# The first norm's root moved behind the first products, with the first two projections walked half by half and the gates' chain turned onto 128 partitions

## The chip, the cores and the metric

The kernel runs on one core of one Trainium2 chip. The core has a matrix engine (PE, with PEld for its weight loads), a vector engine (DVE), a scalar engine (ACT), a general engine (POOL) and a sync engine (SP), which here only issues DMAs. Each engine takes its instructions in the order in which they stand in the program and waits, one instruction at a time, for what they need. The metric is the device time of one execution in microseconds (us), as a median of several runs.

## The reference

A token block of 256 tokens of width 1024 passes one hybrid layer and two further layers. The change touches the beginning of the first:

```python
hdn = rms_norm(x, g_mix_pre)          # x * rsqrt(mean(x^2) + eps) * g
proj = hdn @ w_in                     # 1024 x 3080
aq, ak, av, mq, mk, mv, mo, mi, mf = split(proj)   # 512,512,512,256,256,512,512,4,4
att = causal_attention(rope(aq), rope(ak), av)     # 8 heads of 64
ig, lf = mi + b_igate, log_sigmoid(mf + b_fgate)   # per token and head
hm = mlstm(mq, mk / 8, mv, ig, lf)                 # 4 heads; uses cumsum(lf), running maximum
hm = rms_norm(hm) * g_mlstm_out * sigmoid(mo)
x = x + rms_norm(concat(att, hm) @ w_out, g_mix_post)
x = x + rms_norm(square(relu(rms_norm(x) @ w_up)) @ w_down)
```

After it come two layers with modulation by `ada_w`, differential attention, a convolution branch and a gated MLP of width 2816. All of it is float32.

## The kernel before, in words

**Products.** Every float32 product is made of three fp32r matmuls: high part of the activation by high part of the weight, high by low, low by high (`mm3`, L282 to L284). Where tokens are the stationary side, one matmul is 128 x 512 wide (`mm_tok`); where weights are, 128 x 256 (`mm_col`). The activations stand transposed in a tile `T` (name `hT`), 8 pieces `k` of 128 rows, high and low part.

**The stream of weights.** All large weights come as a list of units of 1 MB (`plan`), in halves of 512 KB. `issue_dma` (L189, on SP) loads a half into one of 8 buffers `raw`. `split` makes of it `whi` on ACT (L199) and `wlo` on POOL (L203) or on DVE (L205); a counter (`rot`) gives three of four to POOL. `pump` steps through the plan as far as the 9 buffers for `whi` and `wlo` let it; each step issues one later DMA. Units of `ada_w` in the plan are no weights for PE: DVE works them off itself (L713).

**Order.** The order on every engine is that of the program's text. Side work is written as generators: queues `fills`, `fills2` and others, of which `tick` takes one step after each used half. So what the text emits beside which half of the weights is set by counts such as `GATES` (steps put before the gates' chain starts).

**The first stage.** SP issues x's first block, the gains' row, 4 halves of `w_in`, x's second block, then more halves; behind 16 halves stand the small loads (positions, norm rows, `dw_conv_w`, the gates' columns `wif`, their biases `bif`, the lambdas), then the stream goes on. Per token block, the norm takes squares and the root (L469, `pre_scale`), multiplies x by it (L474, L475), transposes (L494), multiplies by the gain (L500, L502) and splits into high and low (L552, L553): `pre_trans`. `a2_block` then runs `aq` and `ak`: token block 0 over all 8 halves, then block 1 over the 8 halves that are still held. After it come the blocks `av`, `mq`, `mk`, `mv`, `mo` in the order `ORDER1`.

**Side work of that stage.** `rotary` (L601 on) makes sines and cosines. `setup` (L650 on) transposes the small rows. `mlstm_gates` (L852 on) makes the gates' 36 x 256 product (24 matmuls against `wif`), then the log-sigmoid and its cumulative sum on 4 partitions x 256 tokens on DVE (L867 to L885), two steps of it between other things per used half. `attention1` (L919) makes the scores (L791, L792), the softmax (its last step on DVE is `P`, L945), the transposes of the probabilities (L808) and the products; it starts once `aq` and `ak` are turned by `rope` and transposed (L783). `mlstm` (L954) begins by transposing the gates' two rows.

Of the kernel before, what the change touches and what calls it, by code (L numbers as in the profile page):

```python
# [11 lines left out]
FT = mybir.dt.float32  # L12
# [15 lines left out]
HB, RB, XB = 9, 8, 4  # L28
SLACK = 2
HOLD0, HOLDZ, HOLDF = 8, 8, 7  # L30
# [10 lines left out]
ST = (1, 1, 4, 1)  # L41
EARLY, CHAIN, TWO = 1, 3, 0
GATES = 3
# [12 lines left out]
def tile_hybrid_then_diff(ctx: ExitStack, tc: tile.TileContext, I, out: bass.AP):  # L56
# [232 lines left out]

    def mm_col(o, xT, k, w, kk, cs, start, stop):  # L290
        h, lo = (xT[0], xT[1]) if isinstance(xT, list) else (xT[:, 0], xT[:, 1])
        mm3(o, w[0][:, kk, cs], w[1][:, kk, cs], h[:, k, :], lo[:, k, :], start, stop)

    def a_block(tag, xT):
        acc = [acc_tile(), acc_tile()]
        for i in range(4):
            w = take(tag)
            for kk in range(2):
                k = 2 * i + kk
                for t in range(2):  # L300
                    mm_tok(acc[t], xT, k, t, w, kk, slice(0, 512), k == 0, k == 7)
# [7 lines left out]
    def a2_block(seq, xT, before, evac, hold):  # L309
# [7 lines left out]
        def half(out, t, b, k0, kn, w):  # L317
            for kk in range(kn):
                k = k0 + kk
                mm_tok(out[b][:, 0:1024 // kn], xT, k, t, w, kk, slice(0, 1024 // kn), k == 0, k == 7)  # L320
# [122 lines left out]

    ident = cst.tile([128, 128], FT, name="ident")
# [7 lines left out]
    ones = cst.tile([128, 128], FT, name="ones")  # L452
    V.memset(ones, 1.0)
# [105 lines left out]

    p = ps_tile()  # L560
    T.transpose(p[:, 0:8], row0, ident[0:8, 0:8])
    col0 = cst.tile([128, 8], FT, name="col0")
    V.tensor_copy(col0, p[:, 0:8])
    hT = new_T()
    xn = {0: pre_scale(0, ST[0])}
    pump(ST[1])
    run(pre_trans(0, xn[0], hT, lambda j: col0[:, j:j + 1], None))
    pump(ST[2])
    xn[1] = pre_scale(1, ST[3])

    posi = cst.tile([128, 2, 2], I32, name="posi")
    small(posi[:, 0, :], I["positions"].rearrange("o (t p) -> p (o t)", p=128))
    small(posi[:, 1, :], I["positions_2"].rearrange("o (t p) -> p (o t)", p=128))
    ROW = {}
    n0 = 0
    for nm, src in (("g_mlp_pre", I["g_mlp_pre"]), ("c", I["c_2"]), ("n1", I["norm1_g_2"]),
                    ("n2", I["norm2_g_2"]), ("lg", I["conv_ln_g_2"]), ("lb", I["conv_ln_b_2"]),
                    ("cb", I["dw_conv_b_2"]), ("sg", I["subln_g_2"]), ("go", I["g_mlstm_out"])):
        v = src.rearrange("l (j p) -> (l j) p", p=128)
        small(rows[n0:n0 + v.shape[0], :], v)  # L580
        ROW[nm] = n0
        n0 += v.shape[0]
    small(rowa[0:96, :], I["ada_b_2"].rearrange("l (j p) -> (l j) p", p=128))
    small(crow[0:31], I["dw_conv_w_2"].rearrange("l k o c -> k l (o c)"))
    wv = w1.rearrange("(k p) n -> p k n", p=128)
    small(wif[:, :, 0:4], wv[:, :, 3072:3076])
    small(wif[:, :, 32:36], wv[:, :, 3076:3080])
    bif = cst.tile([4, 2], FT, name="bif")
    small(bif[:, 0:1], I["b_igate"].rearrange("l h -> h l"))
    small(bif[:, 1:2], I["b_fgate"].rearrange("l h -> h l"))  # L590
    for i, nm in enumerate(("lambda_q1_2", "lambda_k1_2", "lambda_q2_2", "lambda_k2_2")):
        src = I[nm]
        small(lamr[:, :, i, :], bass.AP(tensor=src.tensor, offset=src.offset, ap=[[0, 128], [64, 2], [1, 64]]))

    pump(2)
# [5 lines left out]
    def rotary():  # L601
# [25 lines left out]
        for s in range(2):  # L627
# [11 lines left out]
                  for _ in range(2))  # L639
    nlam = cst.tile([128, 2], FT, name="nlam")  # L640
# [9 lines left out]
    def setup():  # L650
        G.memset(mask, 0.0)
# [26 lines left out]
        set_up.append(1)  # L678
        yield
        lst = st_tile()  # L680
# [171 lines left out]
    def mlstm_gates():  # L852
# [7 lines left out]
        gw = xn_tile((4, 4, 256))  # L860
        ig, zf, e, s = (gw[:, i, :] for i in range(4))
        s2 = b = e
# [33 lines left out]
    def evac(t, acc):  # L896
# [8 lines left out]
        if t == 0:  # L905
            fills.append(setup())
# [496 lines left out]
```

## Time and profile before

| | |
|---|---|
| median of 3 runs | 1123.03 us (1116.99, 1123.03, 1123.46) |
| the profiled execution's own time | 1118.56 us |
| its span, first to last instruction | 1116.8 us |
| busy: PE, DVE, ACT, POOL | 94%, 61%, 50%, 63% of the span |
| granted TensorE clock, mean | 0.979 of full speed |

The span is one execution; the 1.8 us beside it are the start and the end around it. An engine's share of the span is a mean over many stages. The stage that the change touches is the first 90 us, and there the idle stretches of PE, and what ended them, say more than the shares.

### The profile page before, as it was taken

What the parts mean: (1) busy time and instruction counts of PE and PEld (TensorE: products, weight loads), DVE (VectorE), ACT (ScalarE), POOL (GpSimd) and SP (SyncE); (2) the same over time, 40 slices, a digit from 0 to 9 for tenths busy, and PEclk for the clock granted to TensorE, in tenths of its full rate; (3) what the DMA queues carried; (4) which work ended last, traced back from release to release, by engine and by line L of the source; (5) the groups of instructions that cost most, each with busy time, mean ns of one, the idle gap of its engine ahead of it and who ended that gap; (6) DMA issues with size and microseconds to landing.
All of it is one profiled execution on the core that took longest, in us unless ns stands there. A gap on an engine that the chain in (4) does not pass through costs nothing.

```text
span 1116.8 us, 17204 instructions
## 1 busy us (share of the span) xinstructions
PE 1052.6 (94%) x6435; PEld 927.4 (83%) x6435; DVE 683.3 (61%) x1161; ACT 559.8 (50%) x931; POOL 709.0 (63%) x419
## 2 busy tenths in 40 slices
PE   5969989999999899989999998989999899999997
PEld 4756778998897778988798998878889888999995
DVE  2694535999964387835569688645875455642323
ACT  5535556434455546674633333446466555443441
POOL 5753455665686597665566655757958467567671
PEclk9988999999999999999999999999999899999998
DMA  9562244999996375454599989836535366775631
GB/s 317 138 205 94 76 156 146 320 337 311 343 314 202 95 207 171 151 170 152 150 310 314 333 317 340 310 131 191 176 125 165 121 197 203 239 246 188 197 108 38
DMA packets 170191, 231.82 MB, mean 208 GB/s; under 512 B 10983, under 2 KB 110525, under 8 KB 170107
## 3 DMA queue, kind: packets, MB, share of 16 engines
q1 hardware_dynamic: 169979, 230.71, 63.1%
q8 instruction: 50, 0.82, 0.3%
q14 instruction: 34, 0.28, 0.1%
q0 software_dynamic: 128, 0.02, 0.0%
HBM read 229.63 MB, written 1.06 MB: 207 GB/s over the span
## 4 chain that ended last, share of the span: by engine, by line
PE 53%; DVE 15%; POOL 9%; issue 8%; ACT 7%; DMA 6%; SPq 1%; POOLq 0%; DVEq 0%; ACTq 0%
PE bank L282 16%; PE bank L283 16%; PE bank L284 16%; POOL wlo L203 8%; DVE bank L713 3%; ACT whi L199 3%; DMA raw<-in_w_ffn_in_dram 3%; DVE wlo L205 2%; DMA raw<-in_w_down_dram 2%; SPq L426 1%; DVE modc L738 1%; ACT xn L469 1%; PE bank L792 1%; PE bank L791 1%; DMA raw<-in_w_ffn_out_dram 1%
## 5 line engine op out<-in xcount | busy, mean ns | idle before, releaser
L203 POOL TENSOR_TENSOR wlo<-raw,whi 128x1024 fp32r<-128x1024 f32 x262 | 653.6, 2518 | 308.2 <-ACT whi L199 271.5
L199 ACT ACTIVATE whi<-raw 128x1024 fp32r<-128x1024 f32 x332 | 337.2, 1053 | 78.6 <-DMA raw<-in_w_ffn_in_dram 28.4
L282 PE MATMUL bank<-T,whi 128*128 128x256 f32 x1072 | 309.4, 289 | 6.0 <-ACT sc L1347 2.8
L284 PE MATMUL bank<-T,wlo 128*128 128x256 f32 x1072 | 304.6, 284 | 0.0
L283 PE MATMUL bank<-T,whi 128*128 128x256 f32 x1072 | 304.5, 284 | 0.0
L282 PEld LDWEIGHTS bank<-T,whi 128*128 128x128 f32 x1072 | 206.4, 193 | 13.8 <-issue 5.9
L283 PEld LDWEIGHTS bank<-T,whi 128*128 128x128 f32 x1072 | 206.5, 193 | 1.1
L284 PEld LDWEIGHTS bank<-T,wlo 128*128 128x128 f32 x1072 | 206.5, 193 | 0.0
L205 DVE TENSOR_TENSOR wlo<-raw,whi 128x1024 fp32r<-128x1024 f32 x70 | 126.3, 1805 | 91.3 <-ACT whi L199 91.0
L283 PE MATMUL bank<-wlo,T 128*128 128x512 f32 (+1 forms) x432 | 170.3, 394 | 11.4 <-POOL wlo L203 11.4
L282 PE MATMUL bank<-whi,T 128*128 128x512 f32 (+1 forms) x432 | 173.6, 402 | 3.0 <-ACT T L552 1.5
L284 PE MATMUL bank<-whi,T 128*128 128x512 f32 (+1 forms) x432 | 169.4, 392 | 0.0
L713 DVE SCALAR_TENSOR_TENSOR bank<-raw,cact,bank 128x512 f32<-128x512 f32 x168 | 126.8, 755 | 7.1 <-DMA raw<-in_ada_w_dram 1.8
L282 PE MATMUL bank<-whi,AB 128*128 128x512 f32 x304 | 120.7, 397 | 0.0
L284 PE MATMUL bank<-whi,AB 128*128 128x512 f32 x304 | 120.0, 395 | 0.0
L283 PE MATMUL bank<-wlo,AB 128*128 128x512 f32 x304 | 119.9, 394 | 0.0
L283 PEld LDWEIGHTS bank<-wlo,T 128*128 128x128 f32 x432 | 82.9, 192 | 29.7 <-POOL wlo L203 14.2
L1155 DVE SCALAR_TENSOR_TENSOR bank<-cu,cw,bank 128x256 f32<-128x256 f32 x232 | 104.4, 486 | 4.1
L282 PEld LDWEIGHTS bank<-whi,T 128*128 128x128 f32 x432 | 82.8, 192 | 23.2 <-ACT T L552 2.9
L284 PEld LDWEIGHTS bank<-whi,T 128*128 128x128 f32 x432 | 82.7, 191 | 17.5 <-DVE T L553 0.5
L552 ACT ACTIVATE AB<-bank 128x512 fp32r<-128x512 f32 (+1 forms) x49 | 26.0, 538 | 108.3 <-DVE bank L1351 63.7
L284 PEld LDWEIGHTS bank<-whi,AB 128*128 128x128 f32 x304 | 57.2, 188 | 13.4
(264 smaller groups left out, 1164.1 us busy)
## 6 DMA issues: line engine op xcount, KB each, us to landing
raw<-in_w_in_dram SPq DMA_DIRECT2D x96, 512.0 KB, 5.1
raw<-in_ada_w_dram SPq DMA_DIRECT2D x96, 512.0 KB, 7.4
raw<-in_w_ffn_in_dram SPq DMA_DIRECT2D x88, 512.0 KB, 4.7
raw<-in_w_ffn_out_dram SPq DMA_DIRECT2D x44, 512.0 KB, 5.2
raw<-in_w_up_dram SPq DMA_DIRECT2D x32, 512.0 KB, 5.5
raw<-in_w_down_dram SPq DMA_DIRECT2D x32, 512.0 KB, 8.4
raw<-in_w_out_dram SPq DMA_DIRECT2D x24, 512.0 KB, 4.4
raw<-in_w_attn_o_dram SPq DMA_DIRECT2D x8, 512.0 KB, 3.3
```

Of the source, the lines that this page charges most:

```text
L199: A.activation(hi, r, AF.Copy)
L203: G.tensor_sub(lo, r, hi.bitcast(FT))
L205: V.tensor_sub(lo, r, hi.bitcast(FT))
L282: T.matmul(o, lh, rh, start=start, stop=False)
L283: T.matmul(o, lh, rl, start=False, stop=False)
L284: T.matmul(o, ll, rh, start=False, stop=stop)
L426: nc.sync.dma_start(dst, src)
L469: A.activation(halves_of(xn)[n], halves_of(x[t])[n], AF.Square, scale=1.0 / 32, accum_out=st[:, n:n + 1])
L552: A.activation(dst_hi, full, AF.Copy)
L713: V.scalar_tensor_tensor(ada["sum"], r[:, kk, :], cact[:, k:k + 1], ada["sum"], op0=OP.mult, op1=OP.add)
L738: V.scalar_tensor_tensor(c, c, 0.0 if vec in (0, 3) else 1.0, adab[:, layer, vec, :], op0=OP.add, op1=OP.add)
L1155: V.scalar_tensor_tensor(ca[:, j, :] if k == 30 else sums[j], cu[:, j, k:k + 256], cw[:, l * 4 + j, k:k + 1], sums[j], op0=OP.mult, op1=OP ...
```

## The change

The norm's root is one number per token, so it can be multiplied onto a product's rows afterwards. x is now transposed as it is (`turn_x`); the gain, one number per row of the transpose, is multiplied while the high and low parts are made (`scale_T`, in pieces of 128 x 128, ACT for the high and DVE for the low part); the root (`root`) comes later, as `r0` by tokens, and for the products that have tokens along the free axis (`mq`, `mk`) as a row `rrow`, spread over the partitions by a matmul. `aq` and `ak` pass half by half with both token blocks. `mm_half` puts the four matmuls with `whi` of a half ahead of the two with `wlo`, here and in all blocks that `a_block` and `a2_block` run in the other layers. Seven matmuls of ones stand at the start. The small loads stand behind the first 8 halves. `rotary` became a part of `setup`. All `wlo` are DVE's until the last half of `ak`. The gates' chain has 128 partitions x 8 columns; the cumulative sum is three small matmuls with a triangle (L931 to L933 of the changed kernel), the running maximum a scan.

```diff
-HB, RB, XB = 9, 8, 4
+HB, RB, XB = 9, 8, 1
...
-ST = (1, 1, 4, 1)
+WARM = 7
...
-GATES = 3
+SETUP, GATES = 3, 1
...
+    def mm_half(o, xT, k0, kn, t, w, cs, start, stop):
+        ts = slice(t * 128, t * 128 + 128)
+        for kk in range(kn):
+            for a in range(2):
+                T.matmul(o, xT[:, a, k0 + kk, ts], w[0][:, kk, cs], start=start and kk == a == 0, stop=False)
+        for kk in range(kn):
+            T.matmul(o, xT[:, 0, k0 + kk, ts], w[1][:, kk, cs], start=False, stop=stop and kk == kn - 1)
...
+    for _ in range(WARM):
+        T.matmul(p[:, 0:128], ones, ones, start=True, stop=True)
...
+    small(crow[0:31], I["dw_conv_w_2"].rearrange("l k o c -> k l (o c)"))
...
+    bif = cst.tile([128, 8], FT, name="bif")
+    for i, nm in enumerate(("b_igate", "b_fgate")):
+        small(bif[:, 4 * i:4 * i + 4], bass.AP(tensor=I[nm].tensor, offset=I[nm].offset, ap=[[0, 128], [1, 4]]))
...
+    def scale_T(t, q):
+        for j in range(4):
+            k, ts = 4 * q + j, slice(t * 128, (t + 1) * 128)
+            scaled_T(hT[:, 0, k, ts], hT[:, 1, k, ts], xt[t, q][:, j * 128:(j + 1) * 128], col0[:, k:k + 1])
+
+    def root(t):
+        st, junk = st_tile(), xn_tile()
+        for n in range(2):
+            square(t, n, junk, st)
+        rstd2(r0[:, t:t + 1], st, 1e-6)
...
+        dg = sc_tile()
+        for t in range(2):
+            A.activation(dg[:, t * 128:(t + 1) * 128], ident, AF.Copy, scale=r0[:, t:t + 1])
         yield
+        p = ps_tile()
+        T.matmul(p[:, 0:256], ones, dg[:, 0:256], start=True, stop=True)
+        A.activation(rrow, p[:, 0:256], AF.Copy)
+        yield from rotary()
...
+        V.tensor_scalar(zn, z, 0.0, None, op0=OP.min)
+        V.scalar_tensor_tensor(na, zn, 2.0, z, op0=OP.mult, op1=OP.subtract)
+        A.activation(e, na, AF.Exp)
         yield
...
         for n in (15, 13, 11, 9, 7, 5, 3):
             V.scalar_tensor_tensor(pl, pl, 1.0 / n, s2, op0=OP.add, op1=OP.mult)
...
+        pb = ps_tile()
+        T.matmul(pb[:, 0:4], tri, lf[:, 0:4], start=True, stop=True)
+        T.matmul(pb[:, 4:8], ones, lf[:, 0:4], start=True, stop=False)
+        T.matmul(pb[:, 4:8], tri, lf[:, 4:8], start=False, stop=True)
...
-    a2_block(pair("aq", "ak"), hT, before, evac, HOLD0)
+    outs = [[acc_tile(), acc_tile()] for _ in range(2)]
+    rot["slack"] = 0
+    for q, (tag, b, k0, kn) in enumerate(pair("aq", "ak")):
+        w = take(tag)
+        for t in range(2):
+            if (q, t) == (0, 1):
+                turn_x(1)
+                scale_T(1, 0)
+                pump(1)
+            mm_half(outs[t][b], hT, k0, kn, t, w, slice(0, 512), k0 == 0, k0 + kn == 8)
+        if q == 1:
+            scale_T(0, 1)
+            scale_T(1, 1)
+        if q in (2, 3):
+            root(q - 2)
+        if q == 7:
+            for t in range(2):
+                evac(t, outs[t])
+            rot["slack"] = SLACK
+            rot["pool"] = POOL
+        done()
...
-            b_block(tag, hT, lambda ps, a=("mq", "mk").index(tag): A.activation(mqk[:, a], ps, AF.Copy))
+            b_block(tag, hT, lambda ps, a=("mq", "mk").index(tag): V.tensor_mul(
+                mqk[:, a], ps, rrow[:, None, :].to_broadcast([128, 2, 256])))
...
-                    A.activation(vt[:, t, :], acc[t], AF.Copy)
+                    A.activation(vt[:, t, :], acc[t], AF.Copy, scale=r0[:, t:t + 1])
```

Three places in the order of the instructions. The first is SP's queue behind the eighth half of `w_in` (`raw_89`), in the changed kernel. `posi`, `T16_71` and `bif` are targets of small loads, `raw` are halves of the stream:

```order
L189 DMA raw_89<-in_w_in_dram 128x2x512
L430 DMA posi_110<-in_positions_dram 128x2x1
...
L430 DMA T16_71<-in_conv_ln_b_2_dram 8x128
...
L430 DMA T16_71<-in_dw_conv_w_2_dram 31x2x512
L430 DMA T16_71<-in_w_in_dram 128x8x4 x2
L430 DMA bif_126<-in_b_igate_dram 128x4
...
L430 DMA T16_71<-in_lambda_k2_2_dram 128x2x64
L189 DMA raw_161<-in_w_in_dram 128x2x512
L189 DMA raw_215<-in_w_in_dram 128x2x512
```

Before, the same small loads stood behind `raw_187`, the sixteenth half; now they stand behind the eighth, and the ninth and tenth half (`raw_161`, `raw_215`) behind them.

The second is ACT at the start, in the changed kernel. `whi` is the high part of a half, `T16_133` the transposed x times the gain; `bank_136` and `bank_193` hold rows 0 to 511 of the transpose of the two token blocks, `bank_141` and `bank_198` rows 512 to 1023:

```order
L589 ACTIVATE T16_133<-bank_193,col0_134 128x128 x4
L199 ACTIVATE whi_211<-raw_77 128x1024
...
L199 ACTIVATE whi_253<-raw_89 128x1024
L199 ACTIVATE whi_259<-raw_161 128x1024
L199 ACTIVATE whi_265<-raw_215 128x1024
L589 ACTIVATE T16_133<-bank_141,col0_134 128x128 x4
L589 ACTIVATE T16_133<-bank_198,col0_134 128x128 x4
L199 ACTIVATE whi_299<-raw_227 128x1024
```

The pieces of `hT` that the fifth to eighth half are multiplied with come behind the high parts of the ninth and tenth half. Before, all pieces of a token block were made together, behind two or eight halves.

The third is PE around the gates' cumulative sum, in the changed kernel (`bank_596`, `bank_597` collect `av`, `xn_509` holds the gates):

```order
L294 MATMUL bank_597<-whi_265,T16_133 128x512 x4
L296 MATMUL bank_597<-wlo_266,T16_133 128x512 x2
L931 MATMUL bank_632<-xn_509 128x4
L932 MATMUL bank_632<-xn_509,ones_91 128x4
L933 MATMUL bank_632<-xn_509 128x4
L294 MATMUL bank_596<-whi_299,T16_133 128x512 x4
```

The three small matmuls need the end of the gates' chain on DVE and stand ahead of the second half of `av`; before, PE had no work of the gates' chain in this place, and none until the mLSTM began.

## Rows read from the trace of the kernel before

**Rows 1.** The page: its first line and the busy times of the engines (us, share of the span, instructions).

```profile
span 1116.8 us, 17204 instructions
...
PE 1052.6 (94%) x6435; PEld 927.4 (83%) x6435; DVE 683.3 (61%) x1161; ACT 559.8 (50%) x931; POOL 709.0 (63%) x419
```

**Rows 2.** The waits of PE over the whole execution: line, what it waited for, us in total, times, the longest.

```profile
PE bank L283 <- POOL wlo L203: 11.4, 8, 1.9
PE bank L808 <- DVE P L945: 10.4, 1, 10.4
```

**Rows 3.** Busy time by stretch of the span (columns in the first line; after the engines the granted TensorE clock, the DMA engines' share and what they moved).

```profile
core 0: us, PE busy (x) PEld busy (x) DVE busy (x) ACT busy (x) POOL busy (x), PEclk, DMA share, GB/s
43.30:46.10 2.80, 2.80 (x26) 2.70 (x25) 0.88 (x3) 0.00 (x0) 2.52 (x7) 1.00 0.81 247
46.10:73.10 27.00, 26.66 (x170) 23.25 (x168) 26.36 (x30) 12.56 (x20) 22.22 (x16) 1.00 0.75 229
83.50:90.50 7.00, 6.96 (x17) 4.87 (x18) 4.73 (x16) 4.85 (x13) 2.38 (x1) 0.50 0.25 77
```

**Rows 4.** PE in order of time: start, duration, instruction, and in brackets the idle time before it and what ended it. The first three are `av`, from 69.18 to 70.03 run a pair of scores, from 70.03 to 72.88 the last of `mk`'s products, L808 transposes probabilities, the last three begin `mv`.

```profile
46.07 0.40 PE L282 MATMUL bank<-whi,T 128*128 128x512 f32 x1
46.30 0.40 PE L283 MATMUL bank<-wlo,T 128*128 128x512 f32 x1
...
69.18 0.48 PE L791 MATMUL bank<-AB 64*128 64x128 f32 x2
...
70.03 0.38 PE L282 MATMUL bank<-T,whi 128*128 128x256 f32 x1
...
72.88 0.28 PE L284 MATMUL bank<-T,wlo 128*128 128x256 f32 x1
83.54 1.08 PE L808 MATMUL bank<-ident,P 128*128 128x128 f32 x3 [10.38 <-DVE P L945]
...
86.13 0.79 PE L282 MATMUL bank<-whi,T 128*128 128x512 f32 x1
86.72 0.63 PE L283 MATMUL bank<-wlo,T 128*128 128x512 f32 x1
87.14 0.63 PE L284 MATMUL bank<-whi,T 128*128 128x512 f32 x1
```

**Rows 5.** DVE in order of time, its work between `av` and `mv`: the gates' chain from its first to its last instruction (L867, L878, L885), the last of them one short step, and four pieces of the modulation (L713).

```profile
57.15 0.99 DVE L867 SCALAR_TENSOR_TENSOR xn<-xn 4x256 f32<-4x256 f32 x1
...
66.22 7.36 DVE L878 SCALAR_TENSOR_TENSOR gm<-gm,xn 4x256 f32<-4x256 f32 x7
73.52 3.11 DVE L713 SCALAR_TENSOR_TENSOR bank<-raw,cact,bank 128x512 f32<-128x512 f32 x4
...
79.30 0.41 DVE L885 TENSOR_TENSOR xn<-xn,gm 4x256 f32<-4x256 f32 x1
```

**Rows 6.** SP's queue in order of time: when an issue began and how long it held the queue. The first row is a half of the first eight, the last one is the first half behind the small loads.

```profile
4.18 0.49 SPq L189 DMA_DIRECT2D raw<-in_w_in_dram  x1
...
28.92 0.28 SPq L426 DMA_DIRECT2D T<-in_conv_ln_b_dram  x1
...
30.85 3.00 SPq L426 DMA_DIRECT2D T<-in_w_in_dram  x2
33.90 3.40 SPq L426 DMA_DIRECT2D bif<-in_b_igate_dram  x1
...
39.71 0.41 SPq L189 DMA_DIRECT2D raw<-in_ada_w_dram  x1
```

**Rows 7.** DMA issues in three narrow windows (KB each, us from issue to landing): the half issued at 4.18, two halves issued at 20.6, and the half issued at 39.71. The last row is what all queues moved from 0 to 60 us, in 40 slices of 1.5 us.

```profile
raw<-in_w_in_dram SPq DMA_DIRECT2D x1, 512.0 KB, 9.3
raw<-in_w_in_dram SPq DMA_DIRECT2D x2, 512.0 KB, 5.1
raw<-in_ada_w_dram SPq DMA_DIRECT2D x1, 512.0 KB, 7.6
GB/s 0 172 332 324 388 374 418 393 391 389 385 385 388 208 147 353 318 299 295 11 38 28 25 47 18 9 37 50 72 219 323 322 277 270 310 172 258 209 217 343
```

**Rows 8.** Durations in the first 60 us: the split on ACT and DVE and a table load on ACT (groups by line and form: count, busy us and mean ns of one); then DVE in order of time: two gains of 128 x 128, four steps at the beginning of `rotary`'s and one at their end, two products of the lambdas (POOL made low parts from 44.84 to 49.59, so beside the first and not beside the second).

```profile
L199 ACT ACTIVATE whi<-raw 128x1024 fp32r<-128x1024 f32 x16 | 16.2, 1050 | 0.8 <-DMA raw<-in_w_in_dram 0.8
L205 DVE TENSOR_TENSOR wlo<-raw,whi 128x1024 fp32r<-128x1024 f32 x4 | 5.3, 1322 | 5.2 <-ACT whi L199 5.2
L628 ACT ACT_TABLE_LOAD x1 | 1.3, 1283 | 0.0
...
9.83 0.75 DVE L500 TENSOR_SCALAR bank<-bank,col 128x128 f32<-128x128 f32 x2 [0.78 <-PE bank L494]
31.32 0.63 DVE L615 TENSOR_SCALAR P<-P 128x8 f32<-128x8 f32 x4
...
33.55 0.18 DVE L626 TENSOR_SCALAR P<-P 128x32 f32<-128x32 f32 x1
...
47.55 2.12 DVE L685 TENSOR_TENSOR T<-T 128x64 f32<-128x64 f32 x1
49.84 0.22 DVE L685 TENSOR_TENSOR T<-T 128x64 f32<-128x64 f32 x1
```

**Rows 9.** PE at two later places where a block of 128 x 512 matmuls waited for a low part.

```profile
370.47 0.79 PE L283 MATMUL bank<-wlo,T 128*128 128x512 f32 x1 [1.93 <-POOL wlo L203]
929.34 0.50 PE L283 MATMUL bank<-wlo,T 128*128 128x512 f32 x1 [1.77 <-POOL wlo L203]
```

More of the change, by code (lines that the diff above doesn't have):

```diff
@@ L297, in a_block @@
             w = take(tag)
[L298 to L301, printed above, removed]
+            for t in range(2):
+                mm_half(acc[t], xT, 2 * i, 2, t, w, slice(0, 512), i == 0, i == 3)
             if i == 3:
@@ L317, in half @@
         def half(out, t, b, k0, kn, w):
-            for kk in range(kn):
-                k = k0 + kk
-                mm_tok(out[b][:, 0:1024 // kn], xT, k, t, w, kk, slice(0, 1024 // kn), k == 0, k == 7)
+            mm_half(out[b][:, 0:1024 // kn], xT, k0, kn, t, w, slice(0, 1024 // kn), k0 == 0, k0 + kn == 8)
         before(0)
@@ L557, in scaled_T, with turn_x @@
         V.scalar_tensor_tensor(dst_lo, full, g, dst_hi.bitcast(FT), op0=OP.mult, op1=OP.subtract)
+    hT = new_T()
+    col0 = cst.tile([128, 8], FT, name="col0")
+    r0 = cst.tile([128, 2], FT, name="r0")
+    xt = {}
+    def turn_x(t):
+        for q in range(2):
+            xt[t, q] = ps_tile()
+            for j in range(4):
+                T.transpose(xt[t, q][:, j * 128:(j + 1) * 128], x[t][:, (4 * q + j) * 128:(4 * q + j + 1) * 128], ident)
+    def scale_T(t, q):
+        for j in range(4):
+            k, ts = 4 * q + j, slice(t * 128, (t + 1) * 128)
+            scaled_T(hT[:, 0, k, ts], hT[:, 1, k, ts], xt[t, q][:, j * 128:(j + 1) * 128], col0[:, k:k + 1])
@@ L571, in tile_hybrid_then_diff @@
[L571 to L593, printed above, removed]
@@ L650, in setup @@
     def setup():
+        for _ in range(SETUP):
+            yield
         G.memset(mask, 0.0)
@@ new lines, in mlstm_gates @@
+        ig, zn, e, s, s2, lf, b = (gw[:, 640 + 8 * i:648 + 8 * i] for i in range(7))
+        z, na, pl = (pg[:, 8 * i:8 * i + 8] for i in range(3))
+        for t in range(2):
+            ts = slice(4 * t, 4 * t + 4)
+            V.scalar_tensor_tensor(ig[:, ts], pt[:, t * 36:t * 36 + 4], r0[:, t:t + 1], bif[:, 0:4],
+                                   op0=OP.mult, op1=OP.add)
+            V.scalar_tensor_tensor(z[:, ts], pt[:, t * 36 + 32:t * 36 + 36], r0[:, t:t + 1], bif[:, 4:8],
+                                   op0=OP.mult, op1=OP.add)
@@ new lines, in mlstm_gates @@
+        V.tensor_sub(u, ig, pb[:, 0:8])
+        A.activation(b, pb[:, 0:8], AF.Copy)
+        yield
+        pm = ps_tile()
+        for t in range(2):
+            T.transpose(pm[0:4, t * 128:(t + 1) * 128], uc[:, 0, t, :], ident)
+        us = gw[0:4, 384:640]
+        A.activation(us, pm[0:4, 0:256], AF.Copy)
+        V.tensor_tensor_scan(gm4, pm[0:4, 0:256], us, 0.0, op0=OP.max, op1=OP.max)
+        yield
+        pm = ps_tile()
+        for t in range(2):
+            T.transpose(pm[:, t * 4:t * 4 + 4], gm4[:, t * 128:(t + 1) * 128], ident[0:4, 0:4])
@@ L890, in tile_hybrid_then_diff @@
+        V.tensor_add(pm[:, 0:8], pm[:, 0:8], b)
+        A.activation(uc[:, 1].rearrange("p t h -> p (t h)"), pm[:, 0:8], AF.Exp, scale=-1.0)
+        yield
+    fills.append(setup())
     fills2.append(mlstm_gates())
[L892 to L894 removed]
     def evac(t, acc):
         for a in range(2):
[L898 removed]
+            A.activation(qk[a][:, t, :], acc[a], AF.Copy, scale=r0[:, t:t + 1])
```

94 lines of the change are left out of this document (47 added, 47 removed).

## The prediction, made before the changed kernel was run

> **What bounds the kernel now.** I read the page first, then PE's waits, then the busy time by stretch, then PE, DVE and SP in order of time. The page [rows 1] shows PE busy for 1052.6 of 1116.8 us, so at most 64 us can be won by removing waits. The reader is to see in the waits [rows 2] that one idle stretch of 10.4 us stands out (L808 for `P`, DVE's last step of the softmax), and that waits of 128 x 512 blocks for a low part make 11.4 us together, in 8 pieces. In PE's order [rows 4] the stretch lies from 73.2 (the end of the row at 72.88) to 83.54. DVE's order [rows 5] says why: the gates' chain holds DVE from 57.15 to 79.7 (22.5 us, with a modulation piece and splits between), and `P` stands behind it. After the stretch PE has a granted clock of 0.50, its 1.2 GHz, up to 90.5 [rows 3]: the pitch of a 128 x 512 matmul is there 0.42 (86.72 to 87.14), against 0.23 at full clock (46.07 to 46.30) [rows 4].
>
> **The point of comparison** is the first matmul of `mv`, 86.13 [rows 4]. From there on both kernels do the same work. 4.4 us of half clock still follow there, which cost half of it, 2.2: 88.3. The old kernel has by then done three pairs of scores at 0.85 (69.18 to 70.03) and transposes of 0.5 (half of the 1.08 at 83.54, which ran at half clock), which the new one does later, as `attention1` starts three steps later: less 3.0, **85.3** is what the new kernel has to beat.
>
> **The start.** Taken away are the two multiplications by the root and PE's wait for them; added are 7 matmuls before anything has landed and so beside the DMAs (cost nothing; without that cover 7 x 0.23 = 1.6, bound 0 to 1.6). Both token blocks pass over the halves as they land, so early on PE has more work per half, and that looks like a gain: the first four halves are done for both blocks by about 21 us (the fourth half's parts exist some 3 us after the one before half 5 lands at 4.18 + 9.3 = 13.5 [rows 6, 7], and two blocks take 12 x 0.23 = 2.8).
>
> But the fifth half needs rows 512 to 1023 of the transposed x, and on ACT these stand behind the high parts of the ninth and tenth half, which SP issues behind all small loads. The eighth half lands at 13.5 + 3 x 1.35 = 17.6 (512 KB at the 388 GB/s of the slices at 7.5 to 18 us [rows 7]). Each issue waits until the DMA eight places ahead has landed: `conv_ln_b` stands eight behind that half. From its issue before (28.92) to the landing of the first half behind the small loads (39.71 + 7.6 = 47.3) it was 18.4 us [rows 6, 7]. So the ninth half lands at 17.6 + 18.4 = 36.0 and the tenth 1.35 later, 37.4. The stretch moved next to nothing while it lasted (9 to 72 GB/s [rows 7]), so it is the issues and round trips that take the time, not bytes. Behind it come the high part (1.05), the low part (1.23, DVE) and the first pieces of `hT` (0.4, one 128 x 128 on DVE being 0.37) [rows 8]: PE begins the fifth half at **40.1**, after an idle time of 19 us. The old kernel had its `aq`/`ak` all but done there (`av` at 46.07 [rows 4]).
>
> The bounds for the tenth half's landing: 29.7 at the least (the two blocked issues of 3.00 and 3.40 taken down to their 0.46 and nothing [rows 6], which leaves 23.2 for the tenth's issue, plus the 5.1 and 1.35 of quickly landing halves [rows 7]), and 39 at the most (the biases now have 128 rows each instead of 4; I put them at one more round trip of half the 3.40). I take 37.4, since it is the same list of loads in the same order.
>
> The Trainium skill, DMA: Bandwidth & Descriptors, section "Anatomy of one DMA", fits one DMA of the GpSimd path as 2.0 us plus bytes over 436 GB/s. By it a half would land 3.2 us after its issue and a load of 64 KB after 2.15, and three rounds of eight small loads would take about 7 us where I count 18.4, an estimate from that page. The landing times of 5.1, 7.6 and 9.3 us for halves on SP's path [rows 7] do not bear it out.
>
> **From the fifth half to `mv`.** PE's work: 48 matmuls of 0.23 (11.0), small transposes 0.9, the gates' product 2.8 (43.30 to 46.10 [rows 3]), `av`, `mq`, `mk` 25.3 (46.10 to 73.10, 27.0, less two pairs of scores of 0.85 that come later [rows 3, 4]), and 1.2 for the small matmuls of the gates: 41.2. The multiplication by `r0` rides on evacuations that were there anyway: nothing, hidden as before. What sets the pace here are two places where PE stands, in order, behind a chain on ACT and DVE.
>
> *The transposes of the gates (before the eighth half).* Their evacuation stands on ACT behind the sines, and these behind `rotary` on DVE. DVE has from 39.7 on: 8 pieces of `hT` at 0.37 (3.0), four low parts at 1.23 (4.9), four modulation pieces (3.11 [rows 5]), `rotary`'s steps (2.4, from 31.32 to 33.73 [rows 8], and 0.3 behind the sines), some 3 of waiting for ACT, which makes the squares, a table load of 1.28 [rows 8] and the high parts in between: 56.5. With sines and evacuation 57.3. PE comes there at 40.1 + 12.0 of work + 3.5 for half clock (7 us at 0.50, as after the idle 10.38 [rows 3, 4]) = 55.6. So **57.3**.
>
> *The cumulative sum (before the second half of `av`'s halves).* From 57.3: transposes 0.3, 23 short steps of the gates on 128 x 8 at 0.22 (5.1), a table load 1.3, three hand-overs to ACT and back at 0.4 (1.2), three low parts (3.7), the lambdas' five short steps (1.1): 12.7, so 70.0. PE has three halves to do, 57.3 + 0.3 + 3 x 2.8 = 66.0, and waits 4.0. The ends for such a step are 0.16 (L615, 128 x 8, four in 0.63) and 0.41 (L885, 4 x 256) [rows 5, 8]; I take 0.22, what L685 needs for 128 x 64 without POOL beside it, since each step here waits for the one before it and some have their operands in the products' banks (`pg`).
>
> From 70.0 PE has the other 20.5 us of the 41.2: `mv` at **90.5**, against 85.3: **+5.2**. The softmax no longer waits for the gates' chain, which is the old 10.4 us gone; the stall of 19 us is what comes in its place.
>
> **The later blocks.** `mm_half` lets four matmuls run before the first low part is needed instead of one: 3 x 0.23 = 0.69 earlier slack per half. Of the eight waits for POOL's low parts [rows 2] four lie behind this stage, in blocks of 128 x 512, each between 1.4 and 1.93 (first and last in [rows 9]) and so longer than 0.69: -2.8. Two more table loads (2.6) lie on ACT, half idle [rows 1]: nothing, 2.6 if that cover is gone.
>
> **Sum:** 1118.56 (the profiled execution) + 5.2 - 2.8 = 1121.0. That execution is 4.5 below the median of the runs shown, so the same change on the median would be 1125.4; I keep to the execution that the durations come from.
>
> **The rivals.**
>
> A: the small loads drain quickly. The tenth half lands at 29.7 and the chains, each started 7.7 earlier, have time to finish beside PE's work. Then `mv` is at 32.4 + 41.2 + 3.5 = 77.1, -8.2, and with -2.8 it is 1107.5; without the half clock, if the idle time is too short for it, 1104. For it: the blocked issues of 3.00 and 3.40 [rows 6] may be due to the two halves of `ada_w` around them. Against: the flat 9 to 72 GB/s [rows 7]. The page named above would give this case. Chance 0.22.
>
> B, the other side: POOL and DVE hold each other up. A step of 128 x 64 took 2.12 while POOL was busy beside it, and 0.22 when it wasn't (L685 [rows 8]). If the gates' 23 steps run at 0.43 instead of 0.22 (+4.8, near L885's price) and two steps of the lambdas at 2.12 (+3.8), the cumulative sum comes at 78.6, PE waits 12.6 there, longer than the 10.38 that brought half clock before [rows 3, 4], which costs another 3.5: `mv` at 102.6, +17.3, less 2.8: 1133. Against it: all low parts are DVE's up to the end of `ak`, so POOL is mostly free in this stage. It decides as soon as the sum starts later than about 77, 11 us behind PE. Chance 0.15.
>
> C: the later waits stay, since the low part's time and not its place decides (POOL is 63% busy [rows 1]): 1118.56 + 5.2 = 1123.8, within my forecast's own range. Chance 0.13, counted with it below.
>
> **How the numbers follow.** The likeliest case has 0.50, with C 0.63, and together they reach from 1113 (the tenth half 5 us earlier, PE's wait halved) to 1128 (the tenth half at 39, steps at 0.3). The predicted time is 1121. The range takes in most of A and B: 1106 to 1133. A measurement of this kernel tells about 1%, 11 us, from no change. A lies at or beyond it, the likeliest case within, B beyond: faster 0.19, same 0.67, slower 0.14.
>
> **What would show it.** In the new trace: PE idle for some 19 us before the fifth half, its releaser ACT's or DVE's piece of `T`, with a DMA of the ninth or tenth half behind it, landing near 36; a granted clock of 0.50 after it; no wait of L808 for `P` of 10 us; a wait of a few us before the three small matmuls of the cumulative sum; shorter waits for POOL's low parts at the places of [rows 9]. I am wrong if PE starts the fifth half before 33 or after 43, or if another wait of over 5 us stands between there and `mv`.

## The result, and the profile after

The changed kernel takes 1129.52 us (median of 7 runs), the kernel before 1121.6 (7 runs): the ratio is 1.0076, 95% interval 1.0053 to 1.0099. By the ratio it is 8.5 us slower (0.0076 of 1120; the medians lie 7.9 apart), and the interval of the ratio is 2.6 us to either side. The forecast was 1121.0, no change that can be told. The profiled executions lie further apart than the medians, 1129.74 against 1118.56, 11.2 us. The page of the changed kernel [rows 1]:

```profile
span 1128.0 us, 17256 instructions
...
PE 1060.3 (94%) x6459; PEld 935.6 (83%) x6459; DVE 675.6 (60%) x1174; ACT 562.6 (50%) x934; POOL 678.7 (60%) x409
```

The waits of PE, whole execution [rows 2]:

```profile
PE bank L294 <- ACT T L589: 13.2, 1, 13.2
PE bank L282 <- ACT AB L585: 6.8, 2, 3.9
PE bank L294 <- ACT whi L199: 6.1, 4, 4.0
PE bank L296 <- POOL wlo L203: 4.2, 4, 1.2
PE bank L713 <- ACT sc L710: 3.8, 1, 3.8
...
PE bank L931 <- DVE xn L927: 3.5, 1, 3.5
```

The wait of 10.4 for the softmax is gone, the eight waits of 11.4 for POOL's low parts are four of 4.2. In their place stands one of 13.2 for a piece of `T`, and two of 3.8 and 3.5 at the diagonal of the root's row and at the cumulative sum. SP's queue, ACT and PE in order of time show how they hang together [rows 4, 6]:

```profile
17.81 0.28 SPq L430 DMA_DIRECT2D T<-in_conv_ln_b_dram  x1
...
22.97 3.48 SPq L430 DMA_DIRECT2D bif<-in_b_igate_dram  x1
...
29.04 8.11 SPq L189 DMA_DIRECT2D raw<-in_w_in_dram  x6
```

```profile
36.46 1.06 ACT L199 ACTIVATE whi<-raw 128x1024 fp32r<-128x1024 f32 x1 [13.77 <-DMA raw<-in_w_in_dram]
37.92 1.06 ACT L199 ACTIVATE whi<-raw 128x1024 fp32r<-128x1024 f32 x1 [0.40 <-DMA raw<-in_w_in_dram]
38.88 0.35 ACT L589 ACTIVATE T<-bank,col 128x128 fp32r<-128x128 f32 x1
40.53 0.37 ACT L589 ACTIVATE T<-bank,col 128x128 fp32r<-128x128 f32 x1 [1.30 <-DVE T L590]
41.32 0.37 ACT L589 ACTIVATE T<-bank,col 128x128 fp32r<-128x128 f32 x1 [0.42 <-DVE T L590]
...
44.98 1.05 ACT L199 ACTIVATE whi<-raw 128x1024 fp32r<-128x1024 f32 x1
...
50.39 1.28 ACT L703 ACT_TABLE_LOAD   x1
...
52.13 0.68 ACT L710 ACTIVATE sc<-ident,r 128x128 f32<-128x128 f32 x2
```

```profile
39.29 0.80 PE L294 MATMUL bank<-whi,T 128*128 128x512 f32 x1 [13.22 <-ACT T L589]
...
52.86 1.22 PE L713 MATMUL bank<-sc,ones 128*128 128x256 f32 x2 [3.76 <-ACT sc L710]
53.52 0.78 PE L282 MATMUL bank<-T,E 128*36 128x256 f32 x1
...
58.95 1.09 PE L294 MATMUL bank<-whi,T 128*128 128x512 f32 x4
...
61.78 0.31 PE L906 MATMUL bank<-ident,xn 36*128 36x36 f32 x2
...
74.03 0.56 PE L931 MATMUL bank<-xn 128*128 128x4 f32 x2 [3.52 <-DVE xn L927]
...
96.58 1.17 PE L294 MATMUL bank<-whi,T 128*128 128x512 f32 x4
```

ACT takes up the ninth half as it lands, at 36.46, and the tenth at 37.92; the pieces of `T` follow, from the second on each 0.79 after the last, then high parts, squares, a table load, and at 52.13 the diagonal of the root's row, for which PE waits at L713. Behind it the gates' 24 products take from 53.52 to 58.95. `mv` begins at 96.58, 10.45 later than before. Of the stretches at a granted clock of 0.50 or 0.51, 1.2 GHz, there are now five in the first 130 us (columns as in [rows 3]):

```profile
7.70:14.50 6.80, 4.98 (x16) 4.15 (x16) 2.28 (x4) 2.08 (x5) 0.00 (x0) 0.50 1.05 394
28.20:45.20 17.00, 5.45 (x12) 3.56 (x12) 4.80 (x10) 4.95 (x11) 0.00 (x0) 0.50 0.80 255
52.00:58.90 6.90, 6.04 (x26) 4.87 (x27) 5.42 (x12) 3.42 (x6) 4.70 (x28) 0.51 0.77 224
72.50:79.40 6.90, 5.38 (x16) 4.54 (x17) 2.56 (x9) 1.12 (x2) 0.83 (x3) 0.51 0.04 7
116.90:127.10 10.20, 10.20 (x30) 7.51 (x30) 2.62 (x11) 3.87 (x13) 4.68 (x4) 0.50 0.16 51
```

Four of them begin inside an idle stretch of PE. In the last PE was busy throughout; an idle stretch of 1.17 had ended just before it, at 116.51. The kernel before has a granted clock of 0.50 twice in its first 150 us: from about 76.9 to 90.5, and from about 134.7 to 138.3, there too with PE busy, behind an idle stretch of 1.01 that ended at 133.35. (Its first products too have the pitch of 1.2 GHz, 0.43 up to about 15 us, though the clock's column reads 1.00 there.)

### The profile page after: what moved, and what is told of

It is laid out like the page before. It is cut to its first block, busy times and chain, and to the rows that moved or that the text cites. A ratio compares the mean times of both kernels' runs of the same rounds, so it can differ in the third digit from the quotient of the medians.

```text
span 1128.0 us, 17256 instructions
## 1 busy us (share of the span) xinstructions
PE 1060.3 (94%) x6459; PEld 935.6 (83%) x6459; DVE 675.6 (60%) x1174; ACT 562.6 (50%) x934; POOL 678.7 (60%) x409
## 4 chain that ended last, share of the span: by engine, by line
PE 57%; DVE 14%; ACT 9%; POOL 7%; DMA 6%; issue 5%; SPq 1%; POOLq 0%; DVEq 0%; ACTq 0%
PE bank L282 14%; PE bank L283 14%; PE bank L284 14%; PE bank L294 7%; POOL wlo L203 5%; PE bank L296 3%; DVE bank L749 3%; ACT whi L199 3%; DVE wlo L205 2%; DMA raw<-in_w_in_dram 2%; DMA raw<-in_w_ffn_in_dram 2%; DMA raw<-in_w_down_dram 2%; ACT xn L502 1%; SPq L430 1%; DVE modc L774 1%
## 5 line engine op out<-in xcount | busy, mean ns | idle before, releaser
L203 POOL TENSOR_TENSOR wlo<-raw,whi 128x1024 fp32r<-128x1024 f32 x250 | 621.9, 2511 | 292.3 <-ACT whi L199 252.4
L294 PE MATMUL bank<-whi,T 128*128 128x512 f32 (+1 forms) x672 | 188.0, 403 | 21.2 <-ACT T L589 13.2
L205 DVE TENSOR_TENSOR wlo<-raw,whi 128x1024 fp32r<-128x1024 f32 x82 | 139.9, 1712 | 105.1 <-ACT whi L199 104.8
L294 PEld LDWEIGHTS bank<-whi,T 128*128 128x128 f32 x672 | 125.5, 194 | 52.1 <-ACT T L589 13.9
L282 PE MATMUL bank<-whi,AB 128*128 128x512 f32 x304 | 119.5, 393 | 0.0
L284 PE MATMUL bank<-whi,AB 128*128 128x512 f32 x304 | 118.4, 390 | 0.0
L296 PE MATMUL bank<-wlo,T 128*128 128x512 f32 (+1 forms) x336 | 105.0, 396 | 4.2 <-POOL wlo L203 4.2
L296 PEld LDWEIGHTS bank<-wlo,T 128*128 128x128 f32 x336 | 63.8, 194 | 19.5 <-POOL wlo L203 6.1
L284 PEld LDWEIGHTS bank<-whi,AB 128*128 128x128 f32 x304 | 57.1, 188 | 12.1
L282 PEld LDWEIGHTS bank<-whi,AB 128*128 128x128 f32 x304 | 57.2, 188 | 11.0
L283 PEld LDWEIGHTS bank<-wlo,AB 128*128 128x128 f32 x304 | 57.2, 188 | 10.9
```

The lines of the kernel that those rows point to most:

```text
L203: G.tensor_sub(lo, r, hi.bitcast(FT))
L205: V.tensor_sub(lo, r, hi.bitcast(FT))
L282: T.matmul(o, lh, rh, start=start, stop=False)
L283: T.matmul(o, lh, rl, start=False, stop=False)
L284: T.matmul(o, ll, rh, start=False, stop=stop)
L294: T.matmul(o, xT[:, a, k0 + kk, ts], w[0][:, kk, cs], start=start and kk == a == 0, stop=False)
```

## The experiments

Times are medians; each ratio is to runs of the kernel before on the same chip. A number of us with a sign is the ratio's distance from 1, times 1120. By the intervals, a difference between two of these ratios is known to some 3 us to either side. The first group changes one thing in the changed kernel, which stands at +8.5, or combines such changes. Line numbers in a row are those of that run's own kernel, so the same instruction can stand some lines further down than in the changed kernel.

**The pieces made early.**

```diff
                 scale_T(1, 0)
+                scale_T(0, 1)
+                scale_T(1, 1)
                 pump(1)
...
-        if q == 1:
-            scale_T(0, 1)
-            scale_T(1, 1)
```

> The changed kernel with one thing moved: the second halves of both transposed token blocks (scale_T for q = 1) are made right behind the first one of block 1, ahead of the high parts of the ninth and tenth half. Theory (the start is held by the ninth and tenth half behind the small loads, and everything that stands behind their high parts on ACT): the idle 13.2 us before the fifth half vanish and PE passes over halves five and six at about 26 to 31 us, but the diagonal for the root's row (L710) stands behind the same high parts, so PE then waits at L713 until about 46.5 instead of 52.9; the gain is the 6.3 us that the eight scaled pieces took on ACT behind the tenth half: 6 us faster than the changed kernel, near 1123. Rival 1 (only the place in ACT's order was wrong, the loads are harmless): the whole 13.2 are won, near 1116. Rival 2 (the loss comes later, from the attention that starts later): no change, near 1129.

Measured: 1124.97, ratio 1.0049 (1.0030 to 1.0068), +5.5: 3.0 faster than the changed kernel where 6 were expected, and so no more than the uncertainty. What the run shows, it shows by its trace. PE in order of time:

```profile
23.27 2.08 PE L294 MATMUL bank<-whi,T 128*128 128x512 f32 x4 [6.15 <-ACT whi L199]
49.67 1.22 PE L713 MATMUL bank<-sc,ones 128*128 128x256 f32 x2 [9.85 <-ACT sc L710]
```

The stall before the fifth half is gone and has moved to L713, where PE now waits 9.85, as the theory said; rival 1, by which the whole stall would be won, is out. But the pieces made early now delay the second half's high part (PE waits 6.15), and the tenth half and all behind it by some 2.5 us.

**The small loads behind ten halves.** (The expectations count 22 small loads; the queue's rows have 21.) The block of `small(...)` calls becomes a function, called once the first half is used:

```diff
+        if q == 0:
+            load_small()
         if q == 1:
```

> The changed kernel with the 22 small loads issued behind ten halves of the weights instead of eight; everything else in its order. Theory: the ninth and tenth half land near 21 us, PE begins the fifth half at about 25 instead of 40; the eleventh half now lands near 39, its high part stands ahead of the squares and the diagonal on ACT, and PE waits for the diagonal at L713 until about 46.7 instead of 52.9: 6 us faster, near 1123. Rival 1 (the ACT order alone): the fifth half still begins as late as the pieces of T can be made, but these no longer wait, so the whole stall is won and no other takes its place, near 1116. Rival 2 (the loss comes later): near 1129.

Measured: 1123.05, ratio 1.0038 (1.0023 to 1.0053), +4.3: 4.2 faster. PE, and the eleventh half's high part on ACT:

```profile
28.72 1.29 PE L294 MATMUL bank<-whi,T 128*128 128x512 f32 x3 [1.33 <-DVE T L592]
...
49.39 1.22 PE L715 MATMUL bank<-sc,ones 128*128 128x256 f32 x2 [12.74 <-ACT sc L712]
```

```profile
41.51 1.06 ACT L199 ACTIVATE whi<-raw 128x1024 fp32r<-128x1024 f32 x1 [8.24 <-DMA raw<-in_w_in_dram]
```

The wait moves in the same way: the first stall shrinks to 1.33, the wait at the diagonal grows from 3.76 to 12.74, since ACT waits for the first half behind the small loads whichever half that is.

**The small loads issued from POOL.**

```diff
+    def small(dst, src):
+        G.dma_start(dst, src)
+
     posi = cst.tile([128, 2, 2], I32, name="posi")
```

> The changed kernel with the 22 small loads issued from POOL instead of SP, nothing else moved. Theory (the small loads cost by standing in SP's queue ahead of the stream, and what is late from them runs through ACT's order): the ninth to eleventh half land near 20 to 23 us, the pieces of T are made from 28 to 33 as in the run with the loads behind ten halves, the eleventh high part follows at 33 instead of 41.5 there, the diagonal for the root's row comes at 41 instead of 52: 10 to 12 us faster than the changed kernel, near 1118. Rival (the loads' bytes and descriptors slow the stream wherever they are issued): at most 5 faster, near 1125.

Measured: 1120.16, ratio 1.0006 (0.9987 to 1.0025): 7.8 faster than the changed kernel, level with the kernel before.

```profile
31.59 0.79 PE L294 MATMUL bank<-whi,T 128*128 128x512 f32 x1 [4.96 <-ACT T L592]
...
45.17 0.70 PE L716 MATMUL bank<-sc,ones 128*128 128x256 f32 x2 [4.38 <-ACT sc L713]
```

This is the largest step of any one edit, and no instruction on ACT, DVE or PE changed its place for it. The loads themselves did: POOL issues the first at 1.89, where SP had issued it at 8.23, so they now run beside the first halves. The gain is less than the 10 to 12 expected: the ninth half still came at 29, not 21. That fits the rival in part (the loads slow the stream wherever they are issued), but no run shows that part by itself.

**The small loads behind 16 halves**, with the early pieces (`pump(6)` ahead of `load_small()`).

> The changed kernel with the small loads behind 16 halves, where they stood before, and the second halves of the transposed blocks made early. Theory: all high parts that ACT has ahead of the diagonal come from the first 14 halves, so no wait for the stream stands before it; the rows it also waits for (the conditioning's column) land near 33 us, the diagonal comes near 41: 10 to 12 us faster than the changed kernel, near 1118. Rival (the small rows themselves, now 7 us later, hold PE at their transposes and then the rest): PE waits over 5 us at L692 and 5 us faster or less.

Measured: 1124.92, ratio 1.0050 (1.0029 to 1.0071), +5.6. The rival holds: now the rows of small values themselves are late, and PE waits 7.47 for them.

```profile
41.27 0.45 PE L694 MATMUL bank<-ident,T 128*128 128x128 f32 x1 [7.47 <-DMA T<-in_ada_b_dram]
```

In the kernel before, with the same place in SP's queue, PE has no wait for any of these rows: it takes them up only behind twelve passes of a token block over a half; here it does so behind eight.

**Off SP, and the pieces early** (both edits above).

> The changed kernel with both: the small loads issued from POOL and the second halves of the transposed blocks made early. Theory: the stream was the cause and ACT's order only its path, so the second edit adds little to the first: within 3 us of the run with the loads off SP alone. Rival (two causes of their own): 6 us faster than it, as the early pieces alone gave 4.6.

Measured: 1115.87, ratio 0.9968 (0.9946 to 0.9989), 4.3 less than without the early pieces. That is between theory (under 3) and rival (6), and with some 3 us of uncertainty the run does not decide between them. That the pieces' place costs something of its own, once the loads are out of the way, is likely by it.

**The pieces batched.**

```diff
         for j in range(4):
-            k, ts = 4 * q + j, slice(t * 128, (t + 1) * 128)
-            scaled_T(hT[:, 0, k, ts], hT[:, 1, k, ts], ...)
+            A.activation(hT[:, 0, k, ts], ..., AF.Copy, scale=col0[:, k:k + 1])
+        for j in range(4):
+            V.scalar_tensor_tensor(hT[:, 1, k, ts], ...)
```

> The changed kernel with the four high pieces of a scale_T issued ahead of the four low ones, instead of in turn. In the changed kernel's trace a piece took 0.79 us, since ACT waited 0.42 for DVE's low piece before each, though it needs nothing from it but the order in which the two engines touch the bank. Theory (in turn is what makes them wait): eight pieces behind the tenth half take 3 us instead of 6.3, the diagonal and all behind it come 3 us earlier: 3 to 4 us faster than the changed kernel, near 1126. Rival (they wait for the shared bank in any order): within 1 us of it, near 1129.5.

Measured: 1124.35, ratio 1.0027 (1.0004 to 1.0049): 5.5 faster than the changed kernel. The eight high pieces behind the tenth half now take 2.15 on ACT, where they took 6.1:

```profile
38.60 2.15 ACT L608 ACTIVATE T<-bank,col 128x128 fp32r<-128x128 f32 x8
```

The wait at L713 is gone; waits of 2.49 and 2.16 at the gates are left. So it was the order in turn that made the two engines wait for each other.

> The changed kernel with the small loads issued from POOL, the second halves of the transposed blocks made early, and the pieces batched. Theory: with the stream free, 16 pieces at 0.79 stand between the first half and the second's high part (PE waited 6.2 us there); batched they take 6 instead of 12.6: 4 to 6 us faster than without the batching, near 1111. Rival (the bank is shared in any order): no change, near 1116.

All three together: 1114.65, ratio 0.9944 (0.9921 to 0.9968), -6.3. The step of 2.7 from the run without batching, where 4 to 6 were expected, lies within the intervals and is not shown. PE still waits 5.67 at the diagonal and 3.38 at the cumulative sum here.

**One matmul of ones** (`WARM = 1`).

> The changed kernel with one matmul of ones at the start instead of seven. Theory (as predicted, they lie beside the first DMAs and cost nothing; and they gain nothing, since the granted clock fell to 0.50 at 7.7 us all the same, after PE had waited): within 2 us of the changed kernel, near 1129.5. Rival (they hold the clock up for the first half): 2 to 4 us slower.

Measured: 1129.39, ratio 1.0067 (1.0046 to 1.0088): no difference, as the theory said.

The second group puts parts of the change alone into the kernel before. **`mm_half`** (in `a_block` and in `a2_block`'s `half`, as in the diff of the change):

> The kernel before with one part of the change alone: mm_half (four matmuls with the high part of a half of the weights ahead of the two with the low part, per token block) in a_block and a2_block. Theory: the eight waits of 11.4 us in all for POOL's low parts lose up to 0.69 each and more where they came in a row: 3 to 5 us faster than before, near 1117. Rival (POOL's time decides and not the place of the low part's use): within 1 us of before, near 1121.

Measured: 1115.8, ratio 0.9963 (0.9945 to 0.9982), -4.1, as the theory said (3 to 5).

**The gates by tokens** (the changed `mlstm_gates`, `bif` and `uc`, with 1.0 for `r0`):

> The kernel before with one part of the change alone: the gates' chain by tokens on 128 partitions, with its small matmuls, begun at the same step as the old chain. Theory: DVE's 22.5 us from L867 to L885 shrink to some 6, L808 no longer waits 10.4 us for the softmax, and the half clock behind that wait (7 us at 0.50, which cost 3.5) goes too; waits of up to 4 us come at the small matmuls: 8 to 12 us faster than before, near 1111. Rival (PE, in order, now waits at the small matmuls for the chain as long as it waited for the softmax): within 3 us of before, near 1121.

Measured: 1114.81, ratio 0.9944 (0.9917 to 0.9972), -6.3, less than the 8 to 12 expected. The softmax's transposes come without a wait, at 78.96 instead of 83.54 [rows 4]:

```profile
53.91 0.31 PE L870 MATMUL bank<-ident,xn 36*128 36x36 f32 x2 [2.57 <-ACT xn L861]
...
78.96 0.49 PE L808 MATMUL bank<-ident,P 128*128 128x128 f32 x3
```

> The kernel before with two parts of the change: mm_half, and the gates' chain by tokens. The norm, its root, the order of the loads and of the first blocks stay as before. Theory: the two gains of 4.1 and 6.3 us that each had alone lie in different places and add up: 9 to 11 us faster than before, near 1110. Rival (the second takes the cover of the first): 6 to 7 faster, no better than the gates alone.

Both: 1112.7, ratio 0.9934 (0.9909 to 0.9959), -7.4. The sum of the two would be 10.4; the difference of 3 is no more than the uncertainty, so whether they add up stays open. The wait for the gates' evacuation is 4.02 here (2.57 above), and the clock is at 0.50 from 52.5 to about 59.3.

**Both, and the gates' chain begun earlier** (`GATES = 1`), then with its sum two steps later:

```diff
+        yield
+        yield
         pb = ps_tile()
```

> The kernel before with both parts as in the run of the two together, and the gates' chain begun two steps earlier (GATES 1). In that run PE waited 4.0 us at the gates' transposes for their evacuation and fell to half clock behind it. Theory: the chain starts while aq and ak still run, the evacuation is no longer late or hides under more products: 2 to 4 us faster than both parts, near 1109. Rival (the evacuation waits for the gates' columns, which land late, wherever it stands): no change, near 1112.7.

Measured: 1114.07, ratio 0.9951 (0.9930 to 0.9972), no gain, but not for the rival's reason. The evacuation is no longer waited for; PE now waits at the next link of the chain, the cumulative sum:

```profile
59.64 0.56 PE L899 MATMUL bank<-xn 128*128 128x4 f32 x2 [6.23 <-DVE xn L895]
```

> The kernel before with both parts and GATES 1, where PE then waited 6.2 us at the small matmuls of the cumulative sum; here these stand two steps later. Theory: neither the transposes (4.0 us in the run of both parts) nor the sum is waited for any more, and the half clock behind them goes: 4 to 6 us faster than both parts, near 1108. Rival (the chain waits on DVE, behind modulation and low parts, for longer than two more steps): within 2 us of both parts.

Measured: **1105.73**, ratio 0.9886 (0.9863 to 0.9908), 12.8 faster than before, the fastest kernel of this study and faster than both given ones. PE meets neither wait (the sum's first matmul at 59.23 stands with no idle time before it):

```profile
45.19 0.31 PE L874 MATMUL bank<-ident,xn 36*128 36x36 f32 x2
59.23 0.28 PE L901 MATMUL bank<-xn 128*128 128x4 f32 x2
```

**Both, and the attention begun three steps later** (a generator of three empty steps ahead of `attention1`).

> The kernel before with both parts of the change (1112.7), and attention1 begun three steps later, as it is in the changed kernel. Theory: the attention's first steps now lie beside mv and mo together with the mLSTM's, where they wait for each other on DVE and ACT; the changed kernel lost some 4 us more behind mv, with a half clock from 117 to 127, and this would be its cause: 3 to 5 us slower than both parts, near 1116.5. Rival (the later attention costs nothing, and what was lost behind mv is the clock's memory of the idle times before it): within 1.5 us of both parts.

Measured: 1113.06, ratio 0.9944 (0.9923 to 0.9965), against 0.9934 of both parts. The rival holds in so far as the later attention costs nothing that can be told; what it says of the clock is not shown by this run.

## Why the prediction was wrong

**The first stall was forecast rightly; the sizes behind it fell short, and one wait stood at another place.** The forecast named the stall before the fifth half, its cause in SP's queue, its path through ACT, the half clock behind it and the two chains at which PE waits. Named landing 36.0 and 37.4; found 36.46 and 37.92. Start of the fifth half 40.1; found 39.29 (first matmul) and 40.55. The list of loads, from `conv_ln_b`'s issue at 17.81, took 18.7 us instead of 18.4. That the loads' place in SP's queue is the largest single cause is shown by the loads issued from POOL: 7.8 us, with intervals that do not touch. None of the signs came that were to refute the forecast: the fifth half began between 33 and 43, and no wait behind it was over 5 us. The loss lies in smaller terms.

The profiled executions are 11.2 apart where 2.4 were forecast, 8.8 more. By PE's rows 4.0 of these had come about at the cumulative sum (74.03 for 70.0), 2.1 between it and `mv`, and 2.7 behind `mv`. "No change that can be told" also rested on 1%, 11 us, as what a measurement tells; the interval was 2.6 us to either side, and 8.5 stood clear of it.

**Three terms of the sum failed, and one held.**

- *"8 pieces of `hT` at 0.37 (3.0)".* On ACT and DVE they took 0.79 each (40.53 to 41.32), 6.1 us from 38.88 to 44.98: high and low part were issued in turn, and ACT waited 0.42 for DVE before most of them. I priced one engine's instruction and not the pair; batching gave 5.5 us back. The wait that came of it was in the wrong place too: the forecast had PE wait at the transposes of the gates, behind DVE, and not at all at the diagonal. PE waited 3.76 at the diagonal (L713), which on ACT stands behind these pieces and behind 7 us of high parts, squares and a table load (44.98 to 52.13). The gates' product behind it took 5.4 at half clock, for the 2.8 of the forecast. So the transposes came at 61.78 instead of 57.3, without a wait of their own.
- *"+3.5 for half clock"*, booked once. The rows show a clock of 0.50 at three waits of PE from the fifth half to `mv`, also at those of under 4 us (52.00 to 58.90, with the idle 3.76 in it; 72.50 to 79.40, with 3.52). Half of PE's busy time in the three stretches is 2.7, 3.0 and 2.7, an estimate of 8.4 in all for the 3.5. From the sum to `mv` PE needed 22.6 us (74.03 to 96.58) for the 20.5 that I had.
- *"From there on both kernels do the same work"*, taken as the same time. Of the last transposes behind the mLSTM, the old kernel's (L1025) began at 150.8, the new one's (L1096) at 167.1, 16.3 later; from 10.45 at `mv`, 3.0 more were foreseen as deferred scores, and 2.2 fewer as half clock that the old kernel still had to pay (its clock was 0.50 to 90.5 [rows 3]). Some 5 were not foreseen, and rows give 4.1 of them. In the new kernel the same work took 10.47 at 1.2 GHz (116.51 to 126.98) and 5.86 at full clock (129.16 to 135.02), 4.6 more; the old kernel lost 1.6 in such a stretch (133.35 to 139.23, 5.88 for the 4.29 of the same work before it). The waits of PE are 4.3 in the new kernel and 3.2 in the old one, 1.1 more.

```profile
116.51 0.49 PE L1070 MATMUL bank<-xn,E 128*128 128x128 f32 x2 [1.17 <-ACT xn L1132]
...
126.98 0.70 PE L1010 MATMUL bank<-P,vt 128*64 128x256 f32 x2
...
129.16 0.49 PE L1070 MATMUL bank<-xn,E 128*128 128x128 f32 x2
...
135.02 0.65 PE L1010 MATMUL bank<-P,vt 128*64 128x256 f32 x2
```

```profile
133.35 0.49 PE L999 MATMUL bank<-xn,E 128*128 128x128 f32 x2 [1.01 <-DVE E L990]
...
139.23 0.65 PE L933 MATMUL bank<-P,vt 128*64 128x256 f32 x2
```

The later attention alone does not do it, by its run. What brings the clock down there stays open: both falls come soon after an idle stretch of about 1 us, but two longer ones in the new kernel, of 1.65 and 1.51 before L1096, brought none. The two groups of transposes (durations in ns, and the first and last start):

```profile
L1025 PE MATMUL bank<-ident,AB x8: 272/272/299, 142.9 to 150.8; 128*128 128x128 f32 x8
```

```profile
L1096 PE MATMUL bank<-ident,AB x8: 272/273/328, 156.9 to 167.1; 128*128 128x128 f32 x8
```

- *"-2.8" for `mm_half`*: right. The four waits behind this stage were 1.93, 1.43, 1.93 and 1.77 before and are 1.23, 0.76, 1.23 and 0.95 now, 2.9 less. (In the kernel before, where it meets all eight waits, it gave 4.1.) First and last, as in [rows 9]:

```profile
386.51 1.21 PE L296 MATMUL bank<-wlo,T 128*128 128x512 f32 x2 [1.23 <-POOL wlo L203]
...
942.44 0.73 PE L296 MATMUL bank<-wlo,T 128*128 128x512 f32 x2 [0.95 <-POOL wlo L203]
```

Two small slips in the working changed nothing: by its terms the lower bound for the tenth half is some 0.3 less than the stated 29.7, and the low part's 1.23 is not the mean of its row in [rows 8], 1.32, which holds one slow instruction; it took 1.23 in the changed kernel.

**The gates' steps** were priced well: 0.22 forecast, seven in 1.43 found, where the old form took 7.36 (L878 [rows 5]):

```profile
72.04 1.43 DVE L925 SCALAR_TENSOR_TENSOR bank<-bank,xn 128x8 f32<-128x8 f32 x7
```

**The rivals.** A (the loads drain quickly) did not happen: the tenth half came at 37.92, not 29.7. The Trainium skill, DMA: Bandwidth & Descriptors, section "Anatomy of one DMA", gives 2 us plus bytes over 436 GB/s for a DMA on the GpSimd path. Read onto this list it would have made A, and the trace does not agree. Issued from POOL, the first small load (`posi`, issued at 1.89) was waited for until 9.27, beside the stream of weights; no run here shows that path with nothing beside it:

```profile
1.89 1.73 POOL L464 DMA_DIRECT2D posi<-in_positions_dram  x2
...
9.27 0.50 POOL L464 DMA_DIRECT2D T<-in_dw_conv_b_dram  x1 [2.62 <-DMA posi<-in_positions_dram]
```

B (POOL and DVE holding each other up in the gates' steps) did not happen either: PE waited 3.52 at the sum, not 12.6. C is out: the later waits did shrink.

**What the change is made of.** Two of its parts are gains, -7.4 together and -12.8 with their places tuned. The rest, the root behind the products with the new start, costs 8.5 + 7.4 = 16 us on top of them as it was written. The loads' place (7.8), the pieces' place (4.3) and their order (2.7, not shown by itself) make 14.8 of it; with all three mended the kernel stands at -6.3, level with the two parts in the old start at -7.4 (the intervals overlap). So with these three mended, moving the root behind the products neither won nor lost anything that can be told. Whether it would win with the gates' steps tuned, as the old start was for its -12.8, was not run: PE still waits for the cumulative sum there. Nor were the other pieces of the new start taken apart, such as the two blocks walked half by half and the low parts all on DVE.

## What to carry to other kernels

A list of small loads in front of a stream holds the stream up, here for the 18.7 us from the issue of `conv_ln_b` to the next landing, and PE stands as soon as the work already loaded runs out, here for 13.2. Count that work in us before moving the list, and follow each engine's order behind the first late transfer, since undoing the first wait alone brought out the next one here (9.85 and 12.74 at the diagonal). Where one engine's step feeds another's on pieces, price the pair as issued, in turn or in groups. Put a small matmul that ends a long chain as many steps later as the chain needs: two empty steps were worth 7.3 us here (0.9886 against 0.9951).

## What the runs showed of the hardware that was not expected

PE's granted clock stood at 0.51 from 72.50 to 79.40, from inside an idle time of 3.52 us on, and at 0.50 through a stretch in which it was busy for 10.20 of 10.20 us (116.90 to 127.10). Seven matmuls of ones at the start, up to 4.4 us, did not keep it up: it stood at 0.50 from 7.70 on, and with one matmul in their place the kernel's time was the same. The same 21 loads cost 7.8 us less issued by POOL than by SP, with the same bytes to the same places, issued from 1.89 on instead of 8.23.
